# A two-layer decoder trunk on one core: squares of the down weights and sums at other places in the feed-forward order, alpha folded into factors, all eight tiles of the next x turned on chip

## The chip, the cores and the metric

The kernel runs on one core of one Trainium2 chip. The metric is the device time of one execution in microseconds (us), the median of several runs.

## What is computed

Two decoder layers over 1024 tokens of width 1024, in float32. Layer 0 mixes tokens by multi-head latent attention (MLA), layer 1 by differential attention. Each mixer and each MLP is followed by a residual with a factor alpha and a layer norm:

```python
for i in range(2):
    m = mla(x, ...) if i == 0 else diff_attn(x, ...)      # each ends in o @ w_o
    x = layernorm(ALPHA * x + m, ln_mix_g[i], ln_mix_b[i])
    x = layernorm(ALPHA * x + square(relu(x @ w_up[i])) @ w_down[i], ln_ffn_g[i], ln_ffn_b[i])
# ALPHA = 4 ** 0.25;  w_up: 1024 x 4096, w_down: 4096 x 1024
# layernorm(x) = (x - mean) * rsqrt(var + LN_EPS) * g + b
```

## The kernel before, in words

**Number format.** Every large product is three float16 products: each operand is scaled and split into a high and a low half (`scaled_split`, L262: ACT writes the high half at L264, DVE the low one at L265), and `mm3` (L185) adds hi*hi, hi*lo and lo*hi in PSUM. The scale of an operand comes from a sum of squares: ACT squares, DVE adds and casts (`total_in`, L269), PE adds over the partitions with a matrix of ones (`total_out`, L274, tiles named tot), and ACT takes the root (`inv_root`, L256). So before a weight can be split, all of it has to be squared once.

**A layer.** After the attention comes the mixer's output product (`out_proj`, L281): for each tile of 128 tokens `start` loads the attention's output and the row of x, POOL multiplies that row by alpha (L320), PE makes the product o, and `end` adds both (`residual`, L230, on DVE with the factor 1/cw that undoes the scale), takes the statistics and the layer norm (`ln_apply`, L247 and L250). Then `mixer_out_and_ffn` (L898) turns the normed tiles by PE (`to_xc`, tiles tp_f) and splits them.

**The MLP** runs by Strassen-Winograd: seven products of half size instead of eight, with sums of blocks made ahead of them. Names end in A in layer 0 and in B in layer 1.

- The up stage has 16 iterations of g (some 18 us each). In each PE makes the products `u_p1` to `u_p7` of g or g+1; ACT copies product 1 from PSUM into the row pu (`u_p1`, L1039), which must be done before product 6 (`u_p6`) overwrites the PSUM tile ab; after product 2 ACT writes a Relu (`u_p2`, L1048). `up_load` (L931) to `up_split` fetch and split up weights for later iterations. `u_out` writes the hidden values h to HBM with POOL's sums of blocks. `wd_scan(g + 1)` (L1115) loads two rows of down weights per iteration (L1121, tiles wds) and ACT squares them at once (L1122); their sums with those of h give the scale of the down product.
- `down_scale` (L1124) makes that scale in two parts: A for the first seven of the eight steps, in iteration 14, and B for all, in the third step of the down stage.
- The down stage has seven products m of eight steps each, 24 matmuls per step and 4 tiles. `d_load` fetches h and down weights ahead, `d_operands` splits them (tiles h16, w16) three steps ahead of their use; the down weights wd pass through a pool of three buffers "raw". After each product `add_y` (L1229) adds it to the rows X2, which were loaded and multiplied by alpha on ACT (L1373). In product 5 rows 0 to 3 are complete and get their layer norm (`fin_stats`, `fin_rstd`, `fin_apply`); rows 4 to 7 get it behind the last product, one after the other.
- In layer 0 the finished rows are turned for the next layer's qkv product: `to_xt` (L1234, tiles tp_n on PE, L216) turns tiles 0 to 2 in product 5 at steps 2, 4 and 6, tile 3 in product 6 at step 1, tiles 4 and 5 behind the last products. Tiles 6 and 7 are stored to HBM, loaded again (L1674) and turned between the qkv groups of the next layer (`transpose_in16`).

**What sets the order.** `in_order()` (L103) keeps PE, DVE, ACT and POOL to the order in which the code of the MLP and the first qkv groups is written; SP, which issues nearly all DMAs, is not bound by it. Elsewhere a scheduler that plans with estimated times places instructions, also between those of the MLP: the scans of the next w_o (`scan`, L295: load of eight rows into "raw", square on ACT, tiles woB0s to woB7s) stand where it puts them, in the kernel before at the beginning of layer 1's attention. Rows of 4 KB per partition live in a pool "X" of eight buffers (wds, pu, h, junk and, in the down stage, X2).

## Time and profile before

| | us |
|---|---|
| median of 3 runs | 2301.41 (2296.93 to 2302.53) |
| profiled execution | 2311.53 |
| its span | 2309.8 |
| up stage, layer 0 and 1 | 515 to 806, 1705 to 1998 |
| down stage, layer 0 and 1 | 806 to 1127, 1998 to 2310 |
| mixer output, layer 0 and 1 | 380 to 497, 1578 to 1688 |

Rows of the profile give a start in us from the span's beginning, a duration, the engine, the line of the kernel, the operation, what it writes and reads, and in brackets the idle time ahead of it with what ended that. PE is the matrix engine, PEld its weight load, DVE the vector engine, ACT the scalar engine, POOL GpSimd, SP the engine that issues DMAs. Buffer numbers are left out of names.

### The profile page before, as it was taken

What the parts mean: (1) busy time and instruction counts of PE and PEld (TensorE: products, weight loads), DVE (VectorE), ACT (ScalarE), POOL (GpSimd) and SP (SyncE); (2) the same over time, 40 slices, a digit from 0 to 9 for tenths busy, and PEclk for the clock granted to TensorE, in tenths of its full rate; (3) what the DMA queues carried; (4) which work ended last, traced back from release to release, by engine and by line L of the source; (5) the groups of instructions that cost most, each with busy time, mean ns of one, the idle gap of its engine ahead of it and who ended that gap; (6) DMA issues with size and microseconds to landing.
All of it is one profiled execution on the core that took longest, in us unless ns stands there. A gap on an engine that the chain in (4) does not pass through costs nothing. (4 is left out here: it accounts for less than half of the span.)

```text
span 2309.8 us, 31741 instructions
## 1 busy us (share of the span) xinstructions
PE 2136.2 (92%) x11255; PEld 1191.6 (52%) x11255; DVE 1684.8 (73%) x2951; ACT 1300.7 (56%) x2400; POOL 529.1 (23%) x381
## 2 busy tenths in 40 slices
PE   7999898989999899999699999969989999999997
PEld 7878775444444344444356655644444444444443
DVE  5677675767777579877578888784857776588787
ACT  5465664446666355446388777673455665354443
POOL 1101001816666310000000001000826666300000
PEclk9999999989999999999899999988989999999999
DMA  4154767526666776652565565455436666856641
GB/s 146 33 104 91 147 123 188 194 101 205 207 213 207 264 281 218 201 192 82 160 155 126 126 122 106 84 118 150 162 142 205 209 210 223 326 198 210 218 155 55
DMA packets 454831, 384.29 MB, mean 166 GB/s; under 512 B 251376, under 2 KB 346624, under 8 KB 454672
## 3 DMA queue, kind: packets, MB, share of 16 engines
q1 hardware_dynamic: 452736, 376.51, 55.2%
q0 software_dynamic: 1936, 5.75, 0.9%
q8 instruction: 88, 1.44, 0.3%
q14 instruction: 71, 0.58, 0.1%
HBM read 247.97 MB, written 83.89 MB: 144 GB/s over the span
## 5 line engine op out<-in xcount | busy, mean ns | idle before, releaser
L185 PE MATMUL yA<-w16A,h16A 128*128 128x512 f16 x1344 | 294.9, 382 | 4.4 <-DVE X2A L1229 3.1
L185 PE MATMUL yB<-w16B,h16B 128*128 128x512 f16 x1344 | 292.8, 380 | 4.6 <-DVE X2B L1229 3.1
L185 PE MATMUL qkv<-wqkv,xt_nA 128*128 128x384 f16 x1536 | 268.5, 328 | 1.0 <-DVE wqkv L265 0.7
L185 PEld LDWEIGHTS <-wuB 128*128 128x128 f16 x1344 | 132.1, 99 | 172.0 <-issue 18.1
L185 PEld LDWEIGHTS <-wuA 128*128 128x128 f16 x1344 | 132.2, 99 | 170.9 <-issue 16.0
L185 PEld LDWEIGHTS <-h16A 128*128 128x128 f16 x1344 | 132.2, 98 | 167.3 <-issue 12.5
L185 PEld LDWEIGHTS <-h16B 128*128 128x128 f16 x1344 | 131.8, 98 | 168.1 <-issue 11.4
L185 PEld LDWEIGHTS <-xt_nA 128*128 128x128 f16 x1536 | 150.0, 99 | 95.8 <-issue 4.4
L1585 DVE TENSOR_REDUCE nmx_d<-ds 128x2 f32<-128x256 f32 (+5 forms) x96 | 90.1, 951 | 24.0 <-PE ds L413 23.6
L265 DVE SCALAR_TENSOR_TENSOR h16B<-hrB,SCB,h16B 128x1024 f16<-128x1024 f32 x56 | 73.3, 1308 | 37.8 <-ACT h16B L264 37.2
L265 DVE SCALAR_TENSOR_TENSOR h16A<-hrA,SCA,h16A 128x1024 f16<-128x1024 f32 x56 | 73.8, 1317 | 35.5 <-ACT h16A L264 35.4
L264 ACT ACTIVATE h16A<-hrA,SCA 128x1024 f16<-128x1024 f32 x56 | 63.9, 1141 | 61.0 <-issue 47.9
L264 ACT ACTIVATE h16B<-hrB,SCB 128x1024 f16<-128x1024 f32 x56 | 63.9, 1140 | 59.9 <-issue 47.9
L413 PE MATMUL s<-kn,qn 128*128 128x512 f32 (+2 forms) x288 | 83.5, 385 | 8.3 <-DVE ph L427 7.8
L185 PE MATMUL oA<-woA,otA 128*128 128x512 f16 x384 | 86.7, 387 | 4.1 <-DVE ph L427 4.1
L185 PE MATMUL oB<-woB,otB 128*128 128x512 f16 x384 | 85.4, 379 | 0.0
L265 DVE SCALAR_TENSOR_TENSOR wuB<-wuB_s,cuB,wuB 128x1024 f16<-128x1024 f32 (+1 forms) x32 | 56.7, 1771 | 34.9 <-ACT wuB L264 34.9
L185 PE MATMUL av_d<-pt16d,dv 128*128 128x256 f16 (+1 forms) x480 | 59.3, 277 | 24.4 <-DMA pt16d<-phd 24.4
L265 DVE SCALAR_TENSOR_TENSOR wuA<-wuA_s,cuA,wuA 128x1024 f16<-128x1024 f32 (+1 forms) x32 | 54.9, 1716 | 34.9 <-ACT wuA L264 34.9
L264 ACT ACTIVATE w16B<-wdB,RBB 128x1024 f16<-128x1024 f32 x40 | 45.7, 1142 | 53.5 <-DVE wdB L1186 53.5
L264 ACT ACTIVATE w16A<-wdA,RBA 128x1024 f16<-128x1024 f32 x40 | 45.7, 1141 | 53.4 <-DVE wdA L1186 53.4
L1489 POOL MEMSET ones_f<- 128x128 f32 x1 | 0.2, 205 | 305.3 <-PE yA L185 305.3
(876 smaller groups left out, 5099.1 us busy)
## 6 DMA issues: line engine op xcount, KB each, us to landing
hrA<-hs_d SPq DMA_DIRECT2D x56, 512.0 KB, 3.8
hrB<-hs_d SPq DMA_DIRECT2D x56, 512.0 KB, 3.8
wuA_r<-in_ffn_w_up_dram SPq DMA_DIRECT2D x32, 512.0 KB, 4.5
wdsA<-in_ffn_w_down_dram SPq DMA_DIRECT2D x32, 512.0 KB, 6.5
wdA<-in_ffn_w_down_dram SPq DMA_DIRECT2D x32, 512.0 KB, 4.7
wuB_r<-in_ffn_w_up_dram SPq DMA_DIRECT2D x32, 512.0 KB, 4.3
wdsB<-in_ffn_w_down_dram SPq DMA_DIRECT2D x32, 512.0 KB, 5.9
wdB<-in_ffn_w_down_dram SPq DMA_DIRECT2D x32, 512.0 KB, 4.6
```

Of the source, the lines that this page charges most:

```text
L185: nc.tensor.matmul(dst, l, r, start=first and m == 0, stop=last and m == n - 1, skip_group_check=resumed)
L264: nc.scalar.mul(hi, src, scale)
L265: nc.vector.scalar_tensor_tensor(out=lo, in0=src, scalar=scale, in1=hi, op0=ALU.mult, op1=ALU.subtract)
L413: nc.tensor.matmul(dst, q_, k_(c0 // 512, n), start=m == 0, stop=m == len(pairs) - 1)
L1489: nc.gpsimd.memset(ones_f, 1.0)
L1585: nc.vector.tensor_reduce(out=nmx[:, ms], in_=st["wide"][:, :, :nk] if i < 4 else st[m], axis=AX.X, op=ALU.max, negate=True)
```

## The change

- The factor alpha is no longer multiplied into x. The factors that undo the scales, icw and icd, are divided by alpha, and the layer norms that follow take LN_EPS / ALPHA ** 2. POOL's L320 and ACT's L1373 go; one or two DVE instructions on 128x1 are added per scale.
- `end` of the mixer's output becomes three steps, `sums`, `squares` and `root`.
- `wd_scan` is split: `wd_fetch(g + 1)` issues the loads where the whole stood; the squares of what was fetched come after product 5, at the end of the iteration.
- `down_sum`, the reduce and the cast, is split from `down_scale` and comes earlier.
- `to_xt` of tiles 0 to 3 comes after (5, 3), (5, 5), (6, 1) and (6, 2) (product, step); tiles 6 and 7 are turned from SBUF behind their layer norm, and the reload goes.

```diff
+    LN_EPS_A = LN_EPS / ALPHA ** 2
...
             nc.vector.reciprocal(icw, cw)
+            nc.vector.tensor_scalar(out=icw, in0=icw, scalar1=1.0 / ALPHA, scalar2=None, op0=ALU.mult)
...
                 nc.sync.dma_start(out=t["x"], in_=x_src[i * P : (i + 1) * P, :])
-                nc.gpsimd.tensor_scalar(out=t["x"], in0=t["x"], scalar1=ALPHA, scalar2=None, op0=ALU.mult)
...
+            def wd_fetch(g):
+                wds[g] = [row(f"wds{nm}{g}{f_}") for f_ in range(2)]
+                for f_ in range(2):
+                    nc.sync.dma_start(out=wds[g][f_], in_=wdn[:, g, f_, :])
             def wd_scan(g):
-                for f_ in range(2):
-                    wr = row(f"wds{nm}{g}{f_}")
-                    nc.sync.dma_start(out=wr, in_=wdn[:, g, f_, :])
+                for f_, wr in enumerate(wds.pop(g)):
                     nc.scalar.activation(wr, wr, AF.Square, accum_out=wdsq[g // 2][:, 2 * (g % 2) + f_ : 2 * (g % 2) + f_ + 1])
...
+            def down_sum(n, key):
+                tsum = fp.tile([P, 1], F32, tag="tsum", name=f"tsum{nm}{key}", bufs=2)
+                nc.vector.tensor_reduce(out=tsum, in_=c1["T"][:, :n], axis=AX.X, op=ALU.add)
+                tb[key] = total_in(tsum, f"cd{nm}{key}")
...
+            wd_fetch(0)
             wd_scan(0)
...
                     if g + 1 < NG:
-                        wd_scan(g + 1)
+                        wd_fetch(g + 1)
                     if w:
                         up_cast(g + 2)
+                    if g == NG - 2:
+                        down_sum(NA, "A")
...
                         u_p5(g + 1)
+                        wd_scan(g + 1)
                     u_out(g)
...
-                    if (m, st_) == (0, 4):
-                        for i in range(NT):
-                            nc.scalar.mul(X[i], X[i], ALPHA)
...
+                    if (m, st_) == (0, 0):
+                        down_sum(NS, "B")
                     if (m, st_) == (0, 2):
                         down_scale(NS, "B")
...
                         if st_ % 2 == 0:
                             fin_stats(i)
-                            if layer == 0 and i > 0:
+                        else:
+                            if layer == 0 and i in (1, 2):
                                 to_xt(xt_n, i - 1, "n", ps_wide)
-                        else:
                             fin_rstd(i)
                             fin_apply(i)
-                    if m == 6 and st_ == 1 and layer == 0:
-                        to_xt(xt_n, 3, "n")
+                    if m == 6 and st_ in (1, 2) and layer == 0:
+                        to_xt(xt_n, 1 + st_, "n")
...
                     fin_rstd(4 + i)
+                if layer == 0:
+                    to_xt(xt_n, 6, "n")
                 fin_apply(7)
+                if layer == 0:
+                    to_xt(xt_n, 7, "n")
...
-            xn = [wp.tile([P, D], F32, tag="raw", name=f"x1_{t}", bufs=3) for t in range(2)]
-            for t in range(2):
-                nc.gpsimd.dma_start(out=xn[t], in_=x1_d[(6 + t) * P : (7 + t) * P, :])
             qkv_load(1)
             for t in range(4):
                 for _, step in qkv_steps(0, t):
                     step()
-                if t in (1, 2):
-                    transpose_in16(xn[t - 1], xt1[1], t + 1, f"nA{5 + t}", sx[:, 2:3])
```

**ACT in the up stage.** The order of ACT in one iteration of layer 0's up stage, from the square of h to the copy pu, before (the numbers in names count tiles):

```order
L1081 ACTIVATE hA_5406,hsA_5552<-hA_5406 128x1024
L264 ACTIVATE wuA_3_5723<-wuA_s_5562,cuA_5652 128x512
L1048 ACTIVATE hA_5738<-abA_5349,cuA_5509 128x512
L1122 ACTIVATE wdsA_5774,wdsqA_5614<-wdsA_5774 128x1024
L1122 ACTIVATE wdsA_5777,wdsqA_5614<-wdsA_5777 128x1024
L1039 ACTIVATE puA_5794<-abA_5379,cuA_5652 128x512
```

and now:

```order
L1090 ACTIVATE hA_5399,hsA_5543<-hA_5399 128x1024
L265 ACTIVATE wuA_3_5713<-wuA_s_5553,cuA_5642 128x512
L1057 ACTIVATE hA_5728<-abA_5342,cuA_5500 128x512
L1136 ACTIVATE wdsA_5607,wdsqA_5743<-wdsA_5607 128x1024
L1136 ACTIVATE wdsA_5608,wdsqA_5743<-wdsA_5608 128x1024
L1048 ACTIVATE puA_5785<-abA_5372,cuA_5642 128x512
```

The squares stand at the same place between the Relu (hA from abA) and pu, but read rows that were allocated one iteration earlier (5607 instead of 5774).

**ACT in product 5 of the down stage of layer 0.** From the operands of step (5, 6) on, before (h16 and w16 are the operands, lj the squares of the layer norm, t_ln and r_ln its root, xt_n the split of a turned tile):

```order
L264 ACTIVATE xt_nA_9498<-tp_nA_9500,xs_c 128x4x128
L264 ACTIVATE xt_nA_9499<-tp_nA_9507,xs_c 128x4x128
L264 ACTIVATE h16A_9543<-hrA_9458,SCA 128x1024
L264 ACTIVATE w16A_9544<-wdA_9460,RBA 128x1024
L160 ACTIVATE t_ln_fA_9551<-y_ln_fA_9549 128x1
L161 ACTIVATE r_ln_fA_9550<-t_ln_fA_9551 128x1
L264 ACTIVATE h16A_9588<-hrA_9514,SCA 128x1024
L264 ACTIVATE w16A_9589<-wdA_9516,RBA 128x1024
L1248 ACTIVATE ljA_9597,fsq_A_9596<-X2A_7914,rsum_fA_9594 128x1024
```

and now:

```order
L265 ACTIVATE h16A_9514<-hrA_9445,SCA 128x1024
L265 ACTIVATE w16A_9515<-wdA_9447,RBA 128x1024
L265 ACTIVATE xt_nA_9520<-tp_nA_9522,xs_c 128x4x128
L265 ACTIVATE xt_nA_9521<-tp_nA_9529,xs_c 128x4x128
L296 ACTIVATE woB0s_raw,fwB<-woB0s_raw,gsub 128x1024
L161 ACTIVATE t_ln_fA_9538<-y_ln_fA_9536 128x1
L162 ACTIVATE r_ln_fA_9537<-t_ln_fA_9538 128x1
L265 ACTIVATE h16A_9575<-hrA_9485,SCA 128x1024
L296 ACTIVATE woB1s_raw,fwB<-woB1s_raw,gsub 128x1024
L296 ACTIVATE woB2s_raw,fwB<-woB2s_raw,gsub 128x1024
L265 ACTIVATE w16A_9576<-wdA_9487,RBA 128x1024
L296 ACTIVATE woB3s_raw,fwB<-woB3s_raw,gsub 128x1024
```

Tile 0's split moves behind the operands of (5, 6), and the scans of w_o, which stood in the attention, now stand among the operands; woB4s to woB7s follow among those of (6, 0) to (6, 2).

**PE at the junction to layer 1.** Behind the last product yA, before:

```order
L185 MATMUL yA_9759<-w16A_9921,h16A_9920 128x512
L216 MATMUL tp_nA_10117<-ident_r,X2A_7920 128x128 x4
L216 MATMUL tp_nA_10124<-ident_r,X2A_7920 128x128 x4
L216 MATMUL tp_nA_10260<-ident_r,x_0_10178 128x128 x4
L216 MATMUL tp_nA_10267<-ident_r,x_0_10178 128x128 x4
L185 LDWEIGHTS xt_nA_9498
L185 MATMUL qkv_2_10274<-wqkv_9846,xt_nA_9498 128x384
```

and now:

```order
L186 MATMUL yA_9732<-w16A_9908,h16A_9907 128x512
L217 MATMUL tp_nA_10104<-ident_r,X2A_7918 128x128 x4
L217 MATMUL tp_nA_10111<-ident_r,X2A_7918 128x128 x4
L217 MATMUL tp_nA_10139<-ident_r,X2A_7920 128x128 x4
L217 MATMUL tp_nA_10146<-ident_r,X2A_7920 128x128 x4
L217 MATMUL tp_nA_10156<-ident_r,X2A_7922 128x128 x4
L217 MATMUL tp_nA_10163<-ident_r,X2A_7922 128x128 x4
L186 LDWEIGHTS xt_nA_9520
L186 MATMUL qkv_2_10271<-wqkv_9819,xt_nA_9520 128x384
```

Tiles 6 and 7 are turned from X2 ahead of qkv_2; before, the reloaded x_0 stood there, and x_1 between qkv_2 and qkv_3.

## Rows read from the trace of the kernel before

**Rows 1.** The page, part 1: engine, busy us (share of the span), instructions.
```profile
PE 2136.2 (92%) x11255; PEld 1191.6 (52%) x11255; DVE 1684.8 (73%) x2951; ACT 1300.7 (56%) x2400; POOL 529.1 (23%) x381
```

**Rows 2.** Windows: us; PE, PEld, DVE, ACT, POOL busy (instructions); clock; DMA share; GB/s.
```profile
515.00:806.00 291.00, 280.10 (x1292) 126.61 (x1291) 199.76 (x294) 172.45 (x279) 176.16 (x110) 0.99 0.64 217
806.00:1097.00 291.00, 281.16 (x1309) 128.44 (x1308) 237.74 (x261) 143.46 (x156) 10.07 (x6) 0.99 0.58 197
```

**Rows 3.** Waits of PE, 515 to 806: what for, us, times, longest.
```profile
PE abA L185 <- ACT puA L1039: 8.7, 6, 4.4
PE tot_cdAA L274 <- DVE totb_cdAA L269: 1.2, 1, 1.2
```

**Rows 4.** Waits of PE, 1705 to 1998.
```profile
PE abB L185 <- ACT puB L1039: 8.3, 5, 4.5
```

**Rows 5.** Timeline, 1752 to 1766.
```profile
1763.12 1.06 ACT L1122 ACTIVATE wdsB<-wdsB 128x1024 f32<-128x1024 f32 x1 [1.64 <-issue]
...
1764.90 1.34 PE L185 MATMUL abB<-xT2B,wuB 128*128 128x512 f16 x5 [1.91 <-ACT puB L1039]
```

**Rows 6.** Timeline of ACT, one iteration later.
```profile
1782.32 0.69 ACT L1039 ACTIVATE puB<-abB,cuB 128x512 f32<-128x512 f32 x1 [0.71 <-PE abB L185]
```

**Rows 7.** Tile wdsA: idle of ACT ahead of its squares, and landing of its loads.
```profile
  issue: 8.8, 10
  DMA wdsA<-in_ffn_w_down_dram: 7.3, 4
...
DMA to landing us min/median/max: 3.4/6.5/8.6
```

**Rows 8.** Timeline of PE, down stage of layer 0, third step.
```profile
826.32 0.16 PE L274 MATMUL tot_cdAB<-totb_cdAB,ones_b 128*128 128x1 bf16 x1 [2.82 <-DVE totb_cdAB L269]
```

**Rows 9.** Waits of PE, 1015 to 1084.
```profile
PE tp_nA L216 <- DVE X2A L250: 5.7, 3, 3.0
```

**Rows 10.** Timeline of ACT, beginning of layer 1's attention.
```profile
1149.68 1.15 ACT L295 ACTIVATE woB1s_raw<-woB1s_raw,gsub 128x1024 f32<-128x1024 f32 x1 [3.62 <-DMA woB1s_raw<-in_diff_w_o_dram]
1150.74 0.19 ACT L295 ACTIVATION_READ_ACCUMULATOR woB1s_raw<-woB1s_raw,gsub 128x1 f32 x1
```

**Rows 11.** The page, part 6: DMA, times, KB, us from issue to landing.
```profile
wdA<-in_ffn_w_down_dram SPq DMA_DIRECT2D x32, 512.0 KB, 4.7
```

**Rows 12.** Timeline of DVE, product 5 of layer 0's down stage.
```profile
1064.97 1.28 DVE L265 SCALAR_TENSOR_TENSOR w16A<-wrA,RBA,w16A 128x1024 f16<-128x1024 f32 x1
```

**Rows 13.** Timeline of PE, 1120 to 1170.
```profile
1142.28 1.94 PE L216 MATMUL tp_nA<-ident_r,x 128*128 128x128 f32 x8 [13.88 <-DMA x<-x_d]
1144.01 6.08 PE L185 MATMUL qkv<-wqkv,xt_nA 128*128 128x384 f16 x24
...
1150.80 4.06 PE L185 MATMUL qkv<-wqkv,xt_nA 128*128 128x384 f16 x24
```

**Rows 14.** Timeline of DVE, 1126 to 1156.
```profile
1136.62 1.28 DVE L250 SCALAR_TENSOR_TENSOR X2A<-X2A,r_ln_fA,lnfbA 128x1024 f32<-128x1024 f32 x1
```

**Rows 15.** Line L320: operation, times, ns min/median/max, first and last start.
```profile
L320 POOL TENSOR_SCALAR XA<-XA x6: 2759/2984/3746, 419.1 to 452.5; 128x1024 f32<-128x1024 f32 x6
```

**Rows 16.** Timeline of DVE, mixer output of both layers.
```profile
485.88 2.37 DVE L250 SCALAR_TENSOR_TENSOR XA<-XA,r_ln_mA,lnmbA 128x1024 f32<-128x1024 f32 x1
...
1680.38 1.28 DVE L250 SCALAR_TENSOR_TENSOR XB<-XB,r_ln_mB,lnmbB 128x1024 f32<-128x1024 f32 x1
1681.58 0.74 DVE L265 SCALAR_TENSOR_TENSOR xT1B<-tp_fB2T,xs_c,xT1B 128x512 f16<-128x512 f32 x1
```

**Rows 17.** Windows, tails of both mixer outputs; columns as in rows 2.
```profile
451.00:497.10 46.10, 34.50 (x170) 19.64 (x169) 40.09 (x63) 18.67 (x35) 19.87 (x13) 0.84 0.20 70
1639.00:1687.80 48.80, 39.91 (x201) 22.42 (x201) 44.06 (x71) 21.32 (x40) 28.89 (x18) 0.89 0.27 98
```

**Rows 18.** Timeline of ACT, 225 to 256.
```profile
230.06 1.15 ACT L295 ACTIVATE woA0s_raw<-woA0s_raw,vf 128x1024 f32<-128x1024 f32 x1 [0.75 <-DMA woA0s_raw<-in_mla_w_o_dram]
...
235.08 1.15 ACT L295 ACTIVATE woA1s_raw<-woA1s_raw,vf 128x1024 f32<-128x1024 f32 x1 [1.97 <-DMA woA1s_raw<-in_mla_w_o_dram]
```

More of the change, by code (lines that the diff above doesn't have):

```diff
@@ L234, in residual, with ln_ssq @@
         return n
-    def ln_stats(xrow, nmean, junk, nm):
+    def ln_ssq(xrow, nmean, junk, nm):
         ssq = sm.tile([P, 1], F32, tag="lnsq", name=f"lnsq_{nm}", bufs=3)
         nc.scalar.activation(junk, xrow, AF.Square, bias=nmean, accum_out=ssq)
-        return rstd_of(ssq, 1.0 / D, LN_EPS, f"ln_{nm}")
+        return ssq
     def ln_apply(dst, xrow, nmean, r, g, b, done=None):
@@ L332, in products, with sums, squares, root @@
                     )
-            def end():
-                nmean = residual(t["y"], icw, t["x"], f"m{nm}{i}")
-                st[i] = t["x"], nmean, ln_stats(t["x"], nmean, t["y"], f"m{nm}{i}")
-            return [(0.1, start)] + [(1.3, lambda k=k: products(k)) for k in range(H)] + [(0.1, end)]
+            def sums():
+                t["m"] = residual(t["y"], icw, t["x"], f"m{nm}{i}")
+            def squares():
+                t["q"] = ln_ssq(t["x"], t["m"], t["y"], f"m{nm}{i}")
+            def root():
+                st[i] = t["x"], t["m"], rstd_of(t["q"], 1.0 / D, LN_EPS_A, f"ln_m{nm}{i}")
+            return (
+                [(0.1, start)]
+                + [(1.3, lambda k=k: products(k)) for k in range(H)]
+                + [(0.1, sums), (0.1, squares), (0.1, root)]
+            )
         return scan, scale, weights, tile_steps, st
@@ L1252, in fin_rstd @@
                 nmean, ssq = fin[i]
[L1253 removed]
+                fin[i] = nmean, rstd_of(ssq, 1.0 / D, LN_EPS_A, f"ln_f{nm}{i}")
             def fin_apply(i):
```

18 lines of the change are left out of this document (11 added, 7 removed).

## The prediction

> **What bounds the kernel now.** I read the page's busy line first [rows 1]: PE is busy 92% of the span. So the time is PE's work, plus the places where PE stands. Then the stages [rows 2]: of 291 us in the up stage of layer 0 PE works 280.1, in the down stage 281.2, at a granted clock of 0.99. A gain there can only come out of some 10 us of idle time in each, which the lists of waits and the timeline name. What the change frees on POOL or ACT away from these waits is worth nothing.
>
> **1. Squares of the down weights on data fetched an iteration earlier (16 us).** In the up stages nearly all of PE's waiting is for pu, ACT's copy of product 1: 8.7 us in six waits in layer 0 [rows 3], 8.3 us in five in layer 1 [rows 4]. The timeline of one iteration shows why [rows 5]: ACT starts the second square only at 1763.12, after standing 1.64 us, and copies pu behind it, so PE starts product 6 at 1764.90, 1.91 us late. In the worst iteration PE stands 4.4 us [rows 3]. One iteration after the first example the same ACT chain runs without a gap, and pu waits for PE instead, 0.71 us [rows 6]. So ACT has the time for the squares, but not for their landing, whose median is 6.5 us [rows 7]. The change leaves the load at its place and squares what was loaded one iteration (about 18 us) earlier; ACT's order is otherwise the same. The buffers are held longer, but the next to use them are pu and junk, which ACT itself writes behind the squares. I take 16 of 17.0, with 12 and 17 as ends: a part of the waits may be for the Relu ahead.
>
> **2. Sums of the scales moved ahead (8 us).** PE waits 1.2 us for totb in each up stage [rows 3], layer 1 alike, and 2.82 us in the third step of each down stage [rows 8]. There two small DVE instructions stand behind an operand split that itself waits for ACT. Both are now issued ahead of such splits. 2 x (1.2 + 2.8) = 8.0. The operands of the next step come when PE needs them by the count of its matmuls, to within 3 us, so ends are 6 and 8.
>
> **3. Transposes of next x half a tile later, and w_o scans that come in (3 us).** In product 5 of layer 0 PE waits three times, 5.7 us in all, for the layer norm of tiles 0 to 2 [rows 9]. The new places are a step of 5.2 us or more later than these waits end, so they go. But in the new ACT order eight squares of w_o stand among the operand splits of steps (5,7) to (6,2); they stood at the beginning of the attention. Each takes 1.34 us (1.15 and 0.19 [rows 10]), and its load goes through three raw buffers, of which one comes free only when the scan or split ahead is done. I walked ACT's queue with 1.14 us for a split, 1.34 for a scan and 4.7 us from issue to landing, as the wd loads have it [rows 11]: operands (6,0) come just in time, (6,1) about 1.2 us late; with landings of 6.5 us [rows 7] 3 to 4 us late. The reserve is small: the split of (6,1) ends at 1066.25 now [rows 12], and PE will want it at about 1068.6. So I take 5.7 less 2.7, that is 3; ends -3 and 5.7.
>
> **4. The junction to layer 1 (4 us).** PE stands 13.88 us for the reload of tile 6 [rows 13]: layer norm, store, load, transpose. Tiles 6 and 7 now come straight from SBUF. Layer norm 7 ends at 1137.90 on DVE now [rows 14]; the two splits of tile 6, of 0.74 us each [rows 16], go ahead of it, and two groups of transposes behind it, so qkv of the second half can start at 1141 to 1143, 1 to 3 us before 1144.01. The transposes between the two qkv groups go too, and ACT's scans, for the load of one of which it stood 3.62 us right here [rows 10], leave the chain to the next scores. I take 4, ends 1 and 7. The 24 matmuls behind the wait take 6.08 us, the next 24 only 4.06 [rows 13]: for a part of them the clock is at its lower level, 1.2 GHz. Idle times of some microseconds stay ahead of them, so I leave these 2.0 us as a cost.
>
> The Trainium skill (TensorE: Matmul & The Clock Gate, HAM oscillation) says that each such wait throws PE back to half clock and that only a loop without the wait keeps the full one. By that the 2.0 us stay, and a wait split in three wins nothing of them; the trace agrees for one long wait, and no row shows three short ones here.
>
> **5. Alpha folded into factors (6.5 us).** The 16 multiplies on ACT, eight at the start of each down stage, have no one that waits for them: 0. The 16 on POOL take 2.76 us and up to 3.75 [rows 15], in the mixer output, where DVE sets the pace of the tail. DVE instructions are longer beside POOL's: the same 128x1024 apply takes 2.37 us at 485.88, 1.28 at 1680.38 [rows 16]. PE stands 46.1 - 34.5 = 11.6 us in the tail of layer 0 and 48.8 - 39.9 = 8.9 in that of layer 1 [rows 17]. Behind the last o product the order before has 12 and 10 groups of transposes left, the new one 7 and 6, each paced by a DVE split of 0.74 us [rows 16]: (5 + 4) x 0.74 = 6.7, and I take 6.5. All the idle would be 20; a third of it surely stays, for the last tile's own layer norm, so ends are 0 and 13. The small DVE instructions that are added stand where 1. and 2. leave room: 0.
>
> **The sum.** 16 + 8 + 3 + 4 + 6.5 = 37.5 us. It is made against the profiled execution, 2311.5 us, 10.1 above the median of the three runs. The waits lie in the program's order, so I take the same difference off the median: 2301.4 - 37.5 = 2263.9, say 2264. All lower ends give 12 + 6 - 3 + 1 + 0 = 16, so 2285; all upper ends 17 + 8 + 5.7 + 7 + 13 = 50.7, so 2251.
>
> **The rivals.**
> - *Mixer output and junction give nothing* (0.16). There PE waits for DVE, whose own work falls little; another of its instructions may end the wait. For it: DVE is busy 40.1 of 46.1 us in the tail [rows 17]. Against it: fewer groups stand behind the last product. Then 16 + 8 + 3 = 27, that is 2274.
> - *Product 6 waits on* (0.12). If pu is late for ACT's Relu and not for the load, 1. gives 4. For it: the tile's view puts 8.8 us down to issue, in ten waits, against 7.3 in four to the load [rows 7]. Against it: the chain without a gap [rows 6]. Then 25.5, that is 2276.
> - *The scans block the operands* (0.05, slower or no gain). ACT works in order, and the eight scans stand ahead of h16 and w16. Layer 0's first scans stand 5.0 us apart, each waiting for its own load [rows 18]. The four steps among which they stand give PE 4 x 5.18 = 20.7 us of work and there are 3 us of reserve, so at a spacing x PE stands 8x - 24: 16 us at 5.0, and above 61.5 / 8 = 7.7 us more than all gains together. At 8.6, the longest landing of the squares' loads [rows 7], it is 45 us, the kernel ends 7 us slower, 2309. Against it: two buffers are free or nearly so when the scans begin, so loads overlap.
> - *Loads are stretched* (0.05). If the scans' loads, on top of hr and wqkv, bring x to 6.5, 28 us of the 37.5 are lost: 2292. The DMA share is 0.58 in that stage and 0.64 where the squares' loads land in 6.5 us [rows 2, 7]. The Trainium skill (DMA: Bandwidth & Descriptors, Issuing engines are not separate DMA queues) has it that all transfers interleave on the same 16 engines; by that a load early in SP's order is no load for nothing.
> - *The change doesn't do what it says* (0.04). The squares keep their place between Relu and pu; if the wait moves to the load of a later row in the same queue, 1. gives nothing and 5. little: some 12 us, 2289.
>
> **How the numbers follow.** The forecast has 0.58. About 0.3% (6.9 us) is what a measurement of this kernel can tell from no change. Slower by more: half of the blocking scans and a little for what I have not seen, 0.03. No difference: the other half and a quarter of the last two cases, 0.05. Faster: 0.92. The range 2250 to 2284 holds the forecast with its bounds and the first two rivals.
>
> **What would show it.** Right: no wait for pu over 0.5 us in the up stages, PE busy some 289 of 291 us there; none for totb; the transposes of tiles 0 to 2 without a wait; none for x at the junction; less than 14 us of idle in the two tails. Wrong: PE waiting for h16 or w16 in steps (6,0) to (6,2) behind the squares of woB, or a new wait at product 6 for the Relu.

## The result

The changed kernel takes 2273.92 us (2272.53 to 2278.35, four runs), the kernel before 2301.97 us (2296.93 to 2305.86) beside it: a ratio of 0.9883, interval 0.9859 to 0.9906. The forecast was 2264 us in a range of 2250 to 2284, with 0.92 for faster. The time lies in the range. Three of the five terms carry the gain; the other two, 7 us by the forecast, brought a loss and nothing.

### The profile page after: what moved, and what is told of

Read it like the earlier page. It is cut to its first block, busy times and chain, and to the rows that moved or that the text cites. A ratio compares the mean times of both kernels' runs of the same rounds, so it can differ in the third digit from the quotient of the medians.

```text
span 2276.2 us, 31758 instructions
## 1 busy us (share of the span) xinstructions
PE 2129.7 (94%) x11255; PEld 1188.6 (52%) x11255; DVE 1678.9 (74%) x2957; ACT 1279.8 (56%) x2384; POOL 487.0 (21%) x363
## 5 line engine op out<-in xcount | busy, mean ns | idle before, releaser
L186 PEld LDWEIGHTS <-xt_nA 128*128 128x128 f16 x1536 | 150.7, 99 | 102.4 <-issue 11.8
L266 DVE SCALAR_TENSOR_TENSOR wuA<-wuA_s,cuA,wuA 128x1024 f16<-128x1024 f32 (+1 forms) x32 | 56.4, 1762 | 35.6 <-ACT wuA L265 20.3
L266 DVE SCALAR_TENSOR_TENSOR wuB<-wuB_s,cuB,wuB 128x1024 f16<-128x1024 f32 (+1 forms) x32 | 55.4, 1731 | 35.6 <-ACT wuB L265 20.3
L186 PE MATMUL av_d<-pt16d,dv 128*128 128x256 f16 (+1 forms) x480 | 59.5, 278 | 21.1 <-DMA pt16d<-phd 21.1
L265 ACT ACTIVATE w16B<-wdB,RBB 128x1024 f16<-128x1024 f32 x40 | 45.6, 1141 | 51.8 <-DVE wdB L1208 51.7
L265 ACT ACTIVATE w16A<-wdA,RBA 128x1024 f16<-128x1024 f32 x40 | 45.6, 1141 | 49.4 <-DVE wdA L1208 49.4
```

Of the source, the lines that this page charges most:

```text
L186: nc.tensor.matmul(dst, l, r, start=first and m == 0, stop=last and m == n - 1, skip_group_check=resumed)
L265: nc.scalar.mul(hi, src, scale)
L266: nc.vector.scalar_tensor_tensor(out=lo, in0=src, scalar=scale, in1=hi, op0=ALU.mult, op1=ALU.subtract)
```

## The profile after

The profiled execution took 2278.35 us with a span of 2276.2, that is 33.6 less than the profiled one of before, where the medians differ by 28.05. The lengths below run from the start or end of one PE row to another (first oA, first product on xT3A, first and last yA, first oB, first on xT3B, first and last yB). "Before, again" is a second profile of the unchanged kernel (run 11 below).

| us | start | mixer output A | up A | down A | junction, attention | mixer output B | up B | down B | span |
|---|---|---|---|---|---|---|---|---|---|
| before | 382.0 | 134.1 | 290.2 | 321.2 | 450.8 | 128.7 | 291.1 | 300.3 | 2309.8 |
| before, again | 381.0 | 133.3 | 287.6 | 321.2 | 450.7 | 129.2 | 287.5 | 300.5 | 2302.2 |
| after | 382.8 | 128.5 | 279.2 | 321.9 | 451.6 | 126.3 | 279.2 | 295.5 | 2276.2 |

Over the runs below, where the work is the same, the up stages and the down stage of layer 1 repeat to 1.3 us, the mixer outputs only to 2.7 and 2.3; the start differs by 2 us and more without cause in the edits. Against the first profile of before the up stages gained 11.0 and 11.9 us, the mixer outputs 5.6 and 2.4, the down stage of layer 1 4.8. The down stage of layer 0 and the junction gained nothing, though 9.8 us were forecast there (3 for transposes and scans, 2.8 of the sums, 4 at the junction).

PE's busy share rose from 92% [rows 1] to 94%, with 6.5 us less of busy time. The page, part 1:

```profile
PE 2129.7 (94%) x11255; PEld 1188.6 (52%) x11255; DVE 1678.9 (74%) x2957; ACT 1279.8 (56%) x2384; POOL 487.0 (21%) x363
```

The up stages by windows, before (two lines) and after (two lines); columns as in [rows 2]:

```profile
516.10:806.40 290.30, 279.40 (x1289) 126.28 (x1288) 199.83 (x293) 172.01 (x279) 176.16 (x110) 0.99 0.64 217
1707.10:1998.20 291.10, 280.01 (x1288) 126.13 (x1287) 202.10 (x293) 170.56 (x277) 175.43 (x110) 0.99 0.63 217
```
```profile
511.30:790.50 279.20, 276.36 (x1289) 124.72 (x1288) 203.83 (x294) 169.69 (x279) 180.96 (x110) 1.00 0.68 226
1690.30:1969.50 279.20, 276.35 (x1289) 124.71 (x1288) 203.82 (x294) 168.61 (x277) 180.91 (x110) 1.00 0.67 226
```

PE's idle time went from 10.9 and 11.1 us to 2.8 each; but PE's busy time, for the same matmuls, fell too, by 3.0 and 3.7, at a granted clock of 1.00 for 0.99. The waits of PE that are left, 511 to 791, answer to [rows 3]: none for pu and none for totb_cd, the cast sums of the down scale. Layer 1 has the same two sizes.

```profile
PE tot_wuA L275 <- DVE totb_wuA L270: 1.6, 4, 1.0
PE abA L186 <- ACT hA L1057: 1.1, 2, 0.6
```

The tile view of wdsA, its idle time and landings, answers to [rows 7]. ACT stands once ahead of a square, for nothing that the profile shows, and never for a load:

```profile
  issue: 1.5, 1
...
DMA to landing us min/median/max: 3.7/5.0/9.0
```

In the down stage of layer 0 the waits for transposes of tiles 0 to 2 are gone [rows 9], and others stand there: ahead of tile 3's transposes (xt_nA is the split of tile 2), for the operand w16 of step (6, 1), and for the split of tile 1. Waits of PE, 1015 to 1084:

```profile
PE tp_nA L217 <- DVE xt_nA L266: 3.9, 1, 3.9
PE yA L186 <- DVE w16A L266: 2.7, 1, 2.7
PE yA L186 <- DVE xt_nA L266: 1.2, 1, 1.2
```

The timeline of ACT shows the w_o squares that came in among the operands. ACT stands 1.55, 4.22 and 1.38 us for their loads, and the operand splits queue behind it:

```profile
1025.34 1.15 ACT L296 ACTIVATE woB0s_raw<-woB0s_raw,gsub 128x1024 f32<-128x1024 f32 x1 [1.55 <-DMA woB0s_raw<-in_diff_w_o_dram]
...
1026.82 1.13 ACT L265 ACTIVATE h16A<-hrA,SCA 128x1024 f16<-128x1024 f32 x1
1032.17 1.15 ACT L296 ACTIVATE woB1s_raw<-woB1s_raw,gsub 128x1024 f32<-128x1024 f32 x1 [4.22 <-DMA woB1s_raw<-in_diff_w_o_dram]
...
1034.53 1.13 ACT L265 ACTIVATE w16A<-wdA,RBA 128x1024 f16<-128x1024 f32 x1
1037.04 1.15 ACT L296 ACTIVATE woB3s_raw<-woB3s_raw,gsub 128x1024 f32<-128x1024 f32 x1 [1.38 <-DMA woB3s_raw<-in_diff_w_o_dram]
```

At the junction the one wait of 13.88 us for the reload [rows 13] became three, 11.91 us in all, two for the layer norms of tiles 6 and 7, and one in qkv_2 for dv, DVE's copy of an earlier qkv group out of PSUM. PE's timeline behind the last product:

```profile
1119.26 1.94 PE L217 MATMUL tp_nA<-ident_r,X2A 128*128 128x128 f32 x8 [5.98 <-DVE y_ln_fA L160]
1125.36 1.94 PE L217 MATMUL tp_nA<-ident_r,X2A 128*128 128x128 f32 x8 [4.17 <-DVE X2A L251]
1129.06 7.11 PE L186 MATMUL qkv<-wqkv,xt_nA 128*128 128x384 f16 x28 [1.76 <-DVE dv L1546]
```

The tails of the two mixer outputs, here the stretches from the last o product to the first up product, by windows, before (two lines) and after (two lines). PE's idle time in them fell from 9.6 and 7.5 us to 7.5 and 3.3, and its instructions from 50 and 40 to 29 and 26, since the planner (the scheduler) now has more transposes ahead of the last o product:

```profile
477.20:497.10 19.90, 10.35 (x50) 7.55 (x48) 17.03 (x24) 8.76 (x15) 8.45 (x6) 0.63 0.13 54
1672.30:1687.80 15.50, 8.01 (x40) 6.15 (x39) 13.91 (x24) 7.39 (x13) 4.88 (x4) 0.66 0.17 68
```
```profile
476.70:490.50 13.80, 6.35 (x29) 4.86 (x30) 12.97 (x24) 6.23 (x11) 2.53 (x2) 0.69 0.31 111
1663.80:1671.10 7.30, 4.00 (x26) 2.79 (x25) 6.55 (x14) 4.70 (x9) 2.53 (x2) 0.92 0.18 72
```

## The experiments

All stand against the kernel before on the same chip; "ratio" is against it. The lengths of their stages, as above:

| us | mixer A | up A | down A | junction, attention | mixer B | up B | down B | median, ratio |
|---|---|---|---|---|---|---|---|---|
| after | 128.5 | 279.2 | 321.9 | 451.6 | 126.3 | 279.2 | 295.5 | 2273.92, 0.9883 |
| 1 scans in the attention | 129.7 | 278.5 | 313.9 | 454.8 | 125.7 | 278.5 | 295.5 | 2274.71, 0.9880 |
| 2 tile 3 in another pool | 127.2 | 278.5 | 318.6 | 451.0 | 126.2 | 279.2 | 295.6 | 2273.89, 0.9881 |
| 3 qkv_2, qkv_3 in the wide pool | 129.6 | 278.5 | 322.2 | 438.5 | 126.6 | 279.2 | 295.5 | 2265.97, 0.9848 |
| 4 squares back behind the loads | 129.1 | 283.7 | 321.6 | 448.7 | 126.5 | 282.1 | 295.5 | 2285.71, 0.9931 |
| 5 sums back | 128.2 | 281.1 | 324.2 | 450.4 | 128.0 | 280.5 | 298.5 | 2287.33, 0.9928 |
| 6 alpha on POOL again | 134.4 | 278.5 | 321.9 | 451.6 | 129.4 | 279.8 | 295.5 | 2285.52, 0.9924 |
| 7 before, with term 1 alone | 134.0 | 280.5 | 321.7 | 453.3 | 129.6 | 280.5 | 300.7 | 2290.87, 0.9952 |
| 8 edits 2 and 3, scans by hand | 129.1 | 279.2 | 314.0 | 438.7 | 126.6 | 278.5 | 295.9 | 2259.14, 0.9807 |
| 9 the same, POOL's sums later | 129.7 | 278.5 | 314.0 | 439.6 | 126.5 | 278.5 | 296.0 | 2257.71, 0.9800 |
| 10 the reload kept | 129.9 | 278.6 | 313.6 | 446.8 | 126.9 | 278.5 | 295.5 | 2264.80, 0.9833 |
| 12 the reload behind qkv_3 | 129.4 | 278.5 | 313.5 | 450.6 | 127.7 | 279.2 | 296.2 | 2269.25, 0.9837 |

The intervals of the ratios are 0.002 to 0.004 wide to each side, so medians less than 5 to 9 us apart tell nothing alone; the stages tell more.

### 1. The w_o scans in the attention

```diff
+            prev = next(i for i in reversed(traced) if i.engine == nc.scalar.engine) if layer == 1 else None
...
+            if prev is not None:
+                ins = next(i for i in reversed(traced) if i.engine == nc.scalar.engine)
+                tc.add_manual_dep(
+                    ins,
+                    prev.name,
+                    mybir.DependencyInfo(mybir.DependencyClass.NoSync, mybir.DependencyReason.DATA),
+                    reason="scan_late",
+                )
...
-            if h == H - 1:
+            if h == 1 and u < 2:
                 steps += [(0.1, lambda k=k: wo_scan(k)) for k in range(4 * u, 4 * u + 4)]
```

> The changed kernel with one difference: the eight squares of layer 1's w_o are tied to ACT's program order in the second head of the attention, so that none stands among the operand splits of layer 0's down stage. Theory A (the scans delay the splits): the waits of PE for w16 (2.7 us), for the split of tile 1 (1.2) and for the split of tile 2 (3.9) in products 5 and 6 go, the down stage of layer 0 is 5 to 8 us shorter than the 321.5 us of the changed kernel from first to last product, and the attention no longer than 2 us more: 2268 to 2272 us in all. Rival B (the new places of the transposes and their PSUM buffers cause the waits, whatever ACT does): the 3.9 us wait stays, the stage is 1 to 4 us shorter, 2271 to 2276 us. Rival C (the scans only move their cost): the attention takes back 4 us or more, 2273 us or over.

Down A got 8.0 us shorter, the stretch with the attention 3.2 longer. PE's waits for w16 and for the split of tile 1 went, but for 0.2 us, as theory A had it; the wait of tile 3's transposes stayed, 3.0 us in place of 3.9, as rival B had it. So the scans are what took most of the gain of down A; moved into the attention, they cost part of it there. The median did not fall, as in rival C.

### 2. Tile 3's transposes in another PSUM pool

```diff
-                        to_xt(xt_n, 1 + st_, "n")
+                        to_xt(xt_n, 1 + st_, "n", None if st_ == 1 else ps_mm)
```

> The changed kernel, but tile 3 is turned in the other PSUM buffers (tag mm), so that it doesn't wait for tile 2's split; the scans stay where they are. Theory B (shared PSUM buffers cause the 3.9 us wait of tile 3): that wait goes, nothing takes its place, 3 to 4 us less, 2270 to 2271 us. Theory A (late splits behind the scans): the wait moves to the next user of those buffers or of the split, and the whole is within 2 us of the changed kernel's 2274.

Down A got 3.3 us shorter, and the median, 2273.89, did not move. Tile 3's transposes no longer wait, but PE stands as long one step later, for totb_wqkv, a cast on DVE that it did not wait for in the changed kernel. PE in the changed kernel and in run 2:

```profile
1068.68 1.77 PE L217 MATMUL tp_nA<-ident_r,X2A 128*128 128x128 f32 x8 [3.86 <-DVE xt_nA L266]
```
```profile
1071.96 0.18 PE L275 MATMUL tot_wqkv<-totb_wqkv,ones_b 128*128 128x4 bf16 x1 [4.71 <-DVE totb_wqkv L270]
```

So the shared PSUM buffers were what held the transposes (tiles 2 and 3, now one step apart, shared two), and freeing them moved the wait, as theory A had it. Of the 3.3 us PE's idle time gives 1.1 (other, smaller waits) and its busy time for the same 1437 matmuls 2.2. The Trainium skill (Perfetto Trace Analysis, Optimization Strategy) names too few PSUM buffers as a possible cause where the same gap repeats; here it was a single gap, and more room moved it on.

### 3. qkv_2 and qkv_3 in the wide pool

```diff
-                qkv_ps[h, i] = ps_mm(f"qkv{h}_{i}")[:, :384]
+                qkv_ps[h, i] = (ps_wide if h == 0 and i in (2, 3) else ps_mm)(f"qkv{h}_{i}")[:, :384]
```

> The changed kernel, but qkv groups 2 and 3 (which need tiles 2 and 3 of x alone) get PSUM buffers of the wide tag, so that they need not wait for groups 0 and 1 to be copied out, and stand on PE ahead of the transposes of tiles 6 and 7. Theory D (the junction is lost because PE's queue has nothing but transposes that wait for layer norms): 96 matmuls of 0.17 us, 8 us, fill idle time of the junction, which loses 5 to 9 us: 2265 to 2269 us. Rival E (the chain from the last layer norm over qkv's copies and the DMA transposes to the first scores sets the time, PE's filling doesn't matter): 0 to 2 us, 2272 to 2274 us.

The stretch got 13.1 us shorter, more than expected, the median 8 us. (The two groups are 48 matmuls, not the 96 of the expectation.) The 24 of qkv_2 now end ahead of the last yA, in what was idle time of down A, whose length stays. PE's timeline at the junction shows the 24 of qkv_3 ahead of the transposes of tiles 6 and 7, which they don't need:

```profile
1114.71 5.74 PE L186 MATMUL qkv<-wqkv,xt_nA 128*128 128x384 f16 x24 [3.12 <-DVE X2A L1251]
1120.29 1.04 PE L217 MATMUL tp_nA<-ident_r,X2A 128*128 128x128 f32 x8
1125.71 1.58 PE L217 MATMUL tp_nA<-ident_r,X2A 128*128 128x128 f32 x8 [4.39 <-DVE X2A L251]
```

### 4. The squares back behind their loads

```diff
                     if g + 1 < NG:
                         wd_fetch(g + 1)
+                        wd_scan(g + 1)
...
-                        wd_scan(g + 1)
```

> The changed kernel with the first part undone: the squares of the down weights stand directly behind their loads, as before. Theory (the load's landing holds ACT's queue and with it pu): the waits for pu come back, 8 to 9 us in each up stage, 2290 to 2293 us. Rival (the wait was the Relu's or came from other edits, the sums moved ahead among them): under 8 us in both stages together, 2282 us or less. As the two up stages together lost 23.0 us and the waits for pu and totb before explain 17.0 + 2.4, some 3 us more may come back with it: then 2294 to 2295.

The waits for pu came back, 5.8 and 3.7 us, not 8.7 and 8.3, and none over 1.6; the median rose by 11.8, to a time between those of theory and rival. Waits of PE in the two up stages:

```profile
PE abA L186 <- ACT puA L1048: 5.8, 7, 1.4
```
```profile
PE abB L186 <- ACT puB L1048: 3.7, 5, 1.6
```

### 5. The sums back at the scale

```diff
-                    if g == NG - 2:
-                        down_sum(NA, "A")
...
                     if g == NG - 2:
+                        down_sum(NA, "A")
                         down_scale(NA, "A")
...
```

and the same for "B", ahead of its scale in the third step of the down stage.

> The changed kernel with down_sum, the reduce and the cast of the down scale, put back to where down_scale stands. Theory (term 2 of the prediction): PE waits for totb come back with the sizes they had before, 1.2 us in each up stage and 2.8 us in each down stage, so about +8 us in all: up stages +1.2 each, down stages +2.8 each in the profile's marks. Rival: what stood behind totb in the down stage was the operands of the next step, which are late anyhow in layer 0 since the w_o scans came in; then layer 0's down stage gains nothing and the sum is +5 us or less. Medians: 2279 to 2282 against 2274.

Up +1.9 and +1.3, down +2.3 and +3.0: the sum is 8.5, as the theory had it. The median is 13.4 us above that of the changed kernel, more than the 5 to 8 expected; no stage places the rest. The waits of the first up stage and of the first down stage:

```profile
PE tot_cdAA L275 <- DVE totb_cdAA L270: 1.2, 1, 1.2
```
```profile
PE tot_cdAB L275 <- DVE totb_cdAB L270: 2.8, 1, 2.8
```

### 6. Alpha on POOL again in the mixer output

```diff
-            nc.vector.tensor_scalar(out=icw, in0=icw, scalar1=1.0 / ALPHA, scalar2=None, op0=ALU.mult)
...
+                nc.gpsimd.tensor_scalar(out=t["x"], in0=t["x"], scalar1=ALPHA, scalar2=None, op0=ALU.mult)
...
-                st[i] = t["x"], t["m"], rstd_of(t["q"], 1.0 / D, LN_EPS_A, f"ln_m{nm}{i}")
+                st[i] = t["x"], t["m"], rstd_of(t["q"], 1.0 / D, LN_EPS, f"ln_m{nm}{i}")
```

> The changed kernel with alpha in the mixer output multiplied into x on POOL again, icw and the epsilon of that layer norm as before; the split of end into sums, squares and root stays, and so does alpha in the MLP's factors. Theory (term 5): the shorter tails of the two mixer outputs, -6.1 and -8.3 us from the last o product to the first up product, came from POOL's multiplies going, so most of it, 10 us or more of 14.4, comes back: 2284 or more. Rival: it is the split of end, and the groups of transposes that the planner moves ahead of the last o product because of it; then 3 us or less come back. A second rival is that POOL's multiplies, where they stand ahead of xsum, make the 4.06 us wait for xsumB longer: the middle of mixer output B, not its tail, gets longer.

The mixer outputs got 5.9 and 3.1 us longer: all that they had gained came back, so it was POOL's multiply and not the split of `end`. Over all profiles, the four with the multiply average 134.0 and 129.2 us and the ten without it 129.0 and 126.7, a difference of 7.4. The tails, by windows, are about as long as before, with 9.3 and 7.8 us of idle PE, and the 48 and 40 PE instructions in them show that the transposes, too, went back behind the last o product:

```profile
477.40:496.90 19.50, 10.25 (x48) 7.49 (x47) 16.69 (x24) 8.76 (x15) 8.45 (x6) 0.63 0.13 54
1662.20:1678.60 16.40, 8.62 (x40) 6.63 (x39) 14.81 (x24) 7.50 (x13) 4.88 (x4) 0.64 0.16 64
```

The second rival fell: no wait for xsumB (POOL's sums of blocks of x) is left in this kernel.

### 7 and 11. Term 1 alone, and the kernel before once more

```diff
+            def wd_fetch(g):
...
                     if g + 1 < NG:
-                        wd_scan(g + 1)
+                        wd_fetch(g + 1)
...
+                        wd_scan(g + 1)
```

> The kernel before with one edit of the change alone: loads of the down weights' rows split from their squares, which come an iteration behind. Theory: the waits for pu go, 17 us by the waits of the kernel before (8.7 and 8.3), that is some 8.5 in each up stage and a median near 2285 against 2302. Rival, from the run in which the squares were put back (9.5 us of waits, 4.5 and 2.9 us longer stages): the edit is worth 7 to 10 us, a median of 2292 to 2295, and the rest of what the up stages gained came with the other edits or from landings that differ from profile to profile. The landings of the squares' loads, median 6.5 us in the kernel before and 5.0 in the changed one, are to be read beside it.

> The kernel before once more, unchanged, for a second profile. Theory: the waits for pu depend on when each load of the down weights' rows lands, which is not the same in each execution, so the profile of before with 17.0 us of them (its span 8 us above the median) shows more than a usual execution: here 7 to 13 us, the up stages 1 to 4 us shorter each. That would explain why the edit alone gave 20.4 us by the two profiles and 11.9 by the medians. Rival: the waits follow from the order of the DMAs alone, and come out as 17 us again, with the same 4.4 us wait at iteration 13.

Against the first profile of before, the up stages of run 7 are 9.7 and 10.6 us shorter, 20.3; against the second, 7.1 and 7.0, that is 14.1; the medians are 11.9 apart, so the time lies between theory and rival, nearer to the rival. No wait for pu is left in run 7. The second profile has 12.6 us of waits for pu, with one of 4.2 us as the longest; the first had 17.0. Its two up stages:

```profile
PE abA L185 <- ACT puA L1039: 6.3, 6, 2.5
```
```profile
PE abB L185 <- ACT puB L1039: 6.3, 5, 4.2
```

The stages from the first mixer output on agree to 0.8 us otherwise. So the waits that term 1 was costed by differ from one execution to the next, as far as two profiles show, and the one at hand had more of them. That the landings of the loads make the difference is argued from [rows 5] and not shown by itself. The edit is worth about 12 us at the median: run 4, which takes it out of the changed kernel, and run 7, which puts it into the other, agree.

### 8 and 9. A combination

Run 8 has edits 2 and 3, and the scans by hand:

```diff
+    at[6, 4] = [lambda k=k: wo_next[0](k) for k in range(3)]
+    at[6, 7] += [lambda k=k: wo_next[0](k) for k in range(3, H)]
...
-            if h == H - 1:
-                steps += [(0.1, lambda k=k: wo_scan(k)) for k in range(4 * u, 4 * u + 4)]
```

> The changed kernel with three edits together: qkv_2 and qkv_3 of layer 1 in the wide PSUM pool instead of the one that the transposes of tiles 6 and 7 use (alone -13.1 us in that stretch of the profile), tile 3's transposes in another PSUM pool (alone -3.3 us in the down stage), and the eight w_o scans put by hand among the operands of product 6, three behind those of step 4 and five behind those of step 7, where they stand behind the last operand splits. Theory: the three add up, since they lie at different places: down stage of layer 0 -8 to -10 us, junction and attention to the first output product -11 to -13, together some 20: a median near 2254. Rival: the scans at the end of the down stage take ACT's time from the chain to the first scores, as they cost 3.7 us when they stood in the attention; then junction and attention win 9 or less, and the median is 2258 to 2262.

Down A -7.9, junction and attention -12.9, together 20.8, as the theory had it; the median, 14.8 below that of the changed kernel, lies where the rival had it, though not for its reason. In down A the gain is no more than that of run 1, the scans alone; but the 24 matmuls of qkv_2 now stand in it, and so does edit 2's wait for totb_wqkv, 3.8 us.

Run 9 adds this in the mixer output:

```diff
                     up_sq(1)
-                    up_add(1)
-                    up_cast(1)
...
                     t = x_sums(i - 4, nc.gpsimd if n < NT - 1 else nc.vector)
+                    if n == 3:
+                        up_add(1)
+                        up_cast(1)
```

> The combination of three edits (wide pool for qkv_2 and qkv_3, tile 3 in another pool, w_o scans by hand), and with it POOL's sums of the second up weight behind xsum of the second pair of tiles in the mixer output, where they stood ahead of it and waited 8 us for a load. Theory: PE's wait for xsumB in mixer output B (4.06 us in the changed kernel, 3.9 in the combination) goes, nothing else moves: 3 to 4 us less than the combination's 2259.1, that is some 2255.5. Rival: the weight's sums come later for the scale of the second iteration, whose operands are then late for the first products, and the tail of the mixer output gives the 3 to 4 us back.

The wait stayed, 3.9 us. POOL's timeline shows why: in layer 1 the planner left the sums of the weight ahead of xsum. (This view puts POOL's 8.04 us down to DVE's xT4B; in run 8 the same gap, 8.06, is put down to the load of the weight.)

```profile
1606.59 1.28 POOL L960 TENSOR_TENSOR wuB_s<-wuB_r 128x512 f32<-128x512 f32 x1 [8.04 <-DVE xT4B L266]
...
1612.61 1.26 POOL L1018 TENSOR_TENSOR xsumB<-XB,XB 128x512 f32<-128x512 f32 x1
```

The edit didn't do what it says, and what the wait is worth stays open. Run 9 is the fastest kernel of this study, but within the spread of run 8.

### 10. The reload kept

```diff
-                if layer == 0:
-                    to_xt(xt_n, 6, "n")
...
-                if layer == 0:
-                    to_xt(xt_n, 7, "n")
...
+            xn = [wp.tile([P, D], F32, tag="raw", name=f"x1_{t}", bufs=3) for t in range(2)]
...
+                if t in (1, 2):
+                    transpose_in16(xn[t - 1], xt1[1], t + 1, f"nA{5 + t}", sx[:, 2:3])
```

> The changed kernel with term 4 undone: tiles 6 and 7 are not turned from SBUF but stored, loaded again and turned between the qkv groups, as before; all else stays. Theory: at the junction the wait for the layer norm took the place of the wait for the reload, so the edit was worth 0 to 1 us: 2274 to 2276 and the stretch from the last product of the down stage to the 48th matmul of the qkv groups changes by less than 1 us. Rival, the prediction's: the edit was worth 4 us and something else of the change cost them again at the junction; then that stretch gets 3 to 5 us longer.

Both were wrong on the time: with the reload kept, the changed kernel is 9.1 us faster. From the last product to the 48th qkv matmul it takes 27.5 us, the changed kernel 27.0, as the theory had it; the wait for the reload is there again. But down A is 8.3 us shorter, with no edit in it, and the stretch with the attention 4.8, for which these runs show no cause. ACT's timeline has the w_o squares at the junction, where they stood before:

```profile
1119.74 1.14 ACT L296 ACTIVATE woB0s_raw<-woB0s_raw,gsub 128x1024 f32<-128x1024 f32 x1
...
1124.50 1.15 ACT L296 ACTIVATE woB1s_raw<-woB1s_raw,gsub 128x1024 f32<-128x1024 f32 x1 [3.53 <-DMA woB1s_raw<-in_diff_w_o_dram]
```

The reloaded rows and the scans take their buffers from the same pool "raw". With the reload gone, nothing of that pool stood between the down stage's weights and the scans, and the planner moved the scans up. That term 4's edit moved them is shown; that it was by the pool's turn is how the code reads.

### 12. The reload behind qkv_3

Run 10 with edits 2 and 3, and the transposes of the reloaded rows written behind the loop over t.

> The kernel with the reload kept (tiles 6 and 7 stored and loaded again, which left the w_o scans in the attention and gave 2264.8), and with it qkv_2 and qkv_3 in the wide PSUM pool, the reload's transposes behind qkv_3 in PE's order instead of ahead of qkv_2 and qkv_3, and tile 3's transposes in another PSUM pool. Theory: the 48 matmuls of qkv_2 and qkv_3 (10 us) now stand ahead of the 14 us wait for the reload and fill it, so the stretch from the last product of the down stage to the first output product of layer 1 gets 8 to 10 us shorter than the 446.8 us with the reload alone, and tile 3's wait of 3.0 us goes from the down stage: 2252 to 2255, faster than the combination with tiles 6 and 7 from SBUF. Rival: the reload is what the first scores of the second half of the tokens wait for, so PE stands as long a little later, behind qkv_3 instead of ahead of it, and the time stays within 4 us of 2264.8.

The rival was nearer, with another place: 2269.25, 4.5 us above run 10. The qkv groups did fill the wait, 5.5 us in place of 14.0, and down A is as long as in run 10 though the 24 matmuls of qkv_2 now end ahead of the last yA. The attention lost what the junction won. Its waits of PE in run 10 and in run 12, each from the last yA to the first oB:

```profile
PE av_d L186 <- DMA pt16d<-phd: 26.5, 13, 5.1
PE tp_nA L217 <- DMA x<-x_d: 14.0, 1, 14.0
```
```profile
PE av_d L186 <- DMA pt16d<-phd: 34.8, 13, 5.2
...
PE tp_nA L217 <- DMA x<-x_d: 5.5, 1, 5.5
```

8.5 us less for the reload, 8.3 more for the turned probabilities pt16d. In run 3, which has the same two qkv groups early, the waits for pt16d rose as well, from 21.1 us in the changed kernel to 28.6, but others of the attention fell, those for p_d on DVE from 10.8 to 4.2. Why not here, these runs don't settle.

## Why the prediction was right and where it was wrong

**Right in the range.** Terms 1, 2 and 5 carry the gain, 30.5 of the 37.5 forecast. Term 3 came out as a loss of some 3.5 us in down A (0.7 lost there, though the sums gave 2.8), term 4 as nothing at the junction, and the runs around them explain most of it. That 28 us still lie in the range is due to its width: it takes in a forecast that is 9.5 too large. (Its upper end, 2284, is 1 us short of the sum of the lower ends, 2285.) The sum was made against one profiled execution and taken off the median; spans of profiles differ by 33.6 us with the first profile of before and by 26.0 with the second. Of the signs named ahead, those for pu, totb, x and tiles 0 to 2 came; the idle time of the two tails is 14.8 us, not under 14, measured as in [rows 17] up to the first up product; and one of the signs of being wrong came too, the wait for w16 in step (6, 1).

**1. Squares (16 forecast).** The mechanism is right: no wait for pu is left, and ACT's squares wait for no load. The size hung on the profiled execution. With this edit alone (run 7) the up stages gain 20.3 and 14.1 us by the two profiles of before, and the median 12. "I take 16 of 17.0" took the waits of one execution, whose own time was 10.1 above the median, for those of the median run. Beyond the waits each profile shows a cost that the sum left out, the clock behind a wait (below). The rival "product 6 waits on" fell: 1.1 us are left for the Relu in each up stage.

**2. Sums (8).** Run 5: 8.5 in the stages, and no wait for totb_cd is left in the changed kernel. Right.

**3. Transposes and scans (3).** The 5.7 us of waits went, as forecast. The step that failed is the walk of ACT's queue, "operands (6,0) come just in time", with 2.7 us as the price of the scans. ACT stood 7.2 us for three of their loads, PE 1.2 and 2.7 us behind them. I had two buffers "free or nearly so" when the scans begin; but SP issued the load of woB1s only at 1026.53, 7.3 us behind that of woB0s, and the two took 5.6 and 6.0 us to land. And the new places of the transposes made a wait that I had no row for, 3.9 us at tile 3, of which 3.0 stay without the scans (runs 1 and 10). The sum then closes: 5.7 of waits gone, 3.9 and 3.9 come, and 1.6 us of PE's busy time at a lower clock make -3.7; with the 2.8 of the sums -0.9, measured -0.7. The stage by windows, before and after:

```profile
806.40:1127.50 321.10, 307.17 (x1437) 141.53 (x1436) 254.47 (x300) 155.46 (x181) 11.14 (x10) 0.99 0.56 189
```
```profile
790.50:1112.40 321.90, 308.75 (x1437) 142.22 (x1436) 253.97 (x302) 157.15 (x189) 10.03 (x6) 0.98 0.62 206
```

With the scans out of the way (runs 1 and 10) down A is 8.0 and 8.3 us shorter. I chose landings of 4.7 us; the bound that I put beside them, 6.5 us with operands "3 to 4 us late", is nearer: the operands of (6, 1) came 2.7 us late, and those 1.2 us that I add to them were PE's wait for a turned tile's split. The rival of the blocking scans had the mechanism, at 16 us and more for it.

**4. The junction (4).** Two steps failed. "qkv of the second half can start at 1141 to 1143": the qkv groups behind the wait are those of tiles 2 and 3, which need neither tile 6 nor tile 7; they stood behind the transposes in PE's order. Run 3 changes nothing but their PSUM pool, which puts them ahead, and that is worth 13.1 us in that stretch. And I took the reload for a wait to be removed. It was also what kept the w_o scans at their place; without it they came into the down stage. Run 10 prices the whole edit: 9.1 us slower than leaving it. Terms 3 and 4 were not two edits with a price each, since the one set the other's order.

**5. Alpha (6.5).** 8.0 in the profile, 7.4 over all profiles, and run 6 shows that POOL's multiplies are the cause. How they lengthen the tail was not as I had it. The last of layer 0's multiplies starts at 452.5 [rows 15], well ahead of the end of the last o product at 477.2; beside the apply of 2.37 us at 485.88 [rows 16] POOL ran a sum of blocks, xsumA at 485.90. In the kernel before the planner had the sums of an up weight ahead of xsumA, POOL stood 15.5 us for their load, and xsumA fell into the tail; without the multiplies xsumA comes first. POOL before and after:

```profile
478.57 1.26 POOL L951 TENSOR_TENSOR wuA_s<-wuA_r 128x512 f32<-128x512 f32 x1 [15.52 <-DMA wuA_r<-in_ffn_w_up_dram]
...
481.13 2.25 POOL L1009 TENSOR_TENSOR xsumA<-XA,XA 128x512 f32<-128x512 f32 x1
```
```profile
467.11 1.27 POOL L1018 TENSOR_TENSOR xsumA<-XA,XA 128x512 f32<-128x512 f32 x1 [11.04 <-PE tp_fA1T L1010]
```

Run 6 has the old order again, with a stand of 15.0 us and xsumA at 480.71. In the tail of layer 0 POOL works 8.45, 2.53 and 8.45 us (before, after, run 6), and DVE takes 17.03, 12.97 and 16.69 us for as many instructions. How much of the gain is this and how much the transposes that moved ahead is not separated. In layer 1 the tail gained 8.2 us and the middle lost 5.8: PE is busy there 3.1 us longer, with the transposes that moved ahead, and idle 2.7 us longer, through one new wait of 4.06. Here the planner moved the sums of an up weight the other way, ahead of xsum, so POOL stands for their load and PE for xsum. PE's row of it in the changed kernel:

```profile
1638.58 1.47 PE L1010 MATMUL tp_fB1T<-ident_r,xsumB 128*128 128x128 f32 x8 [4.06 <-POOL xsumB L1019]
```

The first rival, "mixer output and junction give nothing", had the number, 2274, by luck: the junction gave nothing, as it said, but the mixer outputs gave 8.0, and what else was missing came from terms 1 and 3.

## What to carry to other kernels

An edit that frees a buffer or an engine also frees whatever the planner had queued behind it: compare the whole order of each engine, and price the newcomers where they land. When a stage does not gain what its waits promised, look for the one that moved in, and undo the edits one by one, the ones that look harmless too. Term 5 shows it twice: with the multiplies gone, POOL's sums of weights moved behind xsum in layer 0 and ahead of it in layer 1. Before trusting the size of waits for DMAs, take a second profile of the same kernel.

## What the runs showed of the hardware that was not expected

**The clock behind a wait.** I charged the lower clock at the junction alone. It costs in the up stages too. Behind the longest wait for pu in the up stage of layer 0 in the kernel before, a product of 12 matmuls took 5.28 us, the next 3.21; where no wait stands ahead it is 2.75:

```profile
763.22 5.28 PE L185 MATMUL abA<-xT2A,wuA 128*128 128x512 f16 x12 [4.35 <-ACT puA L1039]
768.29 3.21 PE L185 MATMUL dA<-xT4A,wuA 128*128 128x512 f16 x12
...
1764.90 4.33 PE L185 MATMUL abB<-xT2B,wuB 128*128 128x512 f16 x12 [1.91 <-ACT puB L1039]
```

The granted clock is 0.50, the 1.2 GHz level, from 763.2 to 768.3, and 1.00 from 771.4 on. So a wait of 4.35 us cost about 3 us more. The third line shows a wait of 1.91 us, the first after 20 us without one, and the product behind it is 1.6 us longer. The 6.7 us by which PE's busy time in the two up stages fell between the first profile of before and the one of after fit this. In down A the same holds: run 1 has 4.6 us less of idle time there and 3.4 less of busy time for the same matmuls.

At the junction after, three shorter waits left the clock as low as one long one. Windows over the first two of them and behind the third:

```profile
1117.00:1129.00 12.00, 3.88 (x16) 3.27 (x17) 8.34 (x14) 4.91 (x12) 0.00 (x0) 0.50 0.21 87
1129.06:1134.00 4.94, 4.94 (x16) 2.38 (x16) 1.85 (x6) 0.62 (x1) 0.00 (x0) 0.50 0.20 38
1134.00:1139.40 5.40, 5.40 (x37) 3.27 (x35) 0.29 (x1) 0.55 (x2) 0.00 (x0) 1.00 0.21 41
```

The 48 matmuls of qkv_2 and qkv_3 take 10.4 us, before 6.08 + 4.06 = 10.1 [rows 13]. The Trainium skill (TensorE: Matmul & The Clock Gate, HAM oscillation) has it that in a loop with such a wait in each round PE starts each round at half clock again. The trace agrees in that the clock did not come back between the three, 0.50 from 1117 to 1134; which of them would have sufficed it does not tell.

**One kernel, two sets of waits.** Two profiles of the same program agree to 1.0 us in the start and to 0.8 in every stage but the up stages, where 17.0 and 12.6 us of waits for pu make 2.6 and 3.6 us of difference.
